# A two-layer decoder trunk: layer 0's small steps at fixed places between the large matmuls, large buffers at multiples of 512 bytes, and natural row order in the output projection

## The chip, the cores and the metric

The kernel runs on one core of a Trainium2 chip. The metric is the time of one execution in microseconds (us); less is better. A core has a matmul engine, TensorE (PE in the profile, with its weight loads on a row of their own, PEld), a vector engine (DVE), a scalar engine (ACT), GpSimd (POOL) and SyncE (SP), which here only issues DMAs. Matmuls read on-chip memory (128 partitions of bytes, in which each buffer has an address) and write to PSUM, a small memory in banks of 512 float32 values per partition.

## What is computed

256 tokens of width 2048 run through two layers. Layer 0 mixes tokens with two kinds of heads, whose inputs come from one projection of 6144 columns:

```python
proj = h @ w_in                      # columns: x, y (recurrence), q, f, v, g (heads), 1024 each
lru = rg_lru(causal_depthwise_conv(x), ...)      # h_t = a_t h_(t-1) + u_t, gates from 256-wide blocks
lru = lru * gelu(y)
hg = hgrn2(q, f, v, ...)             # 8 heads of 128; per-head RMSNorm; times silu(g)
mixed = concat(lru, hg) @ w_out      # 2048 x 2048
h = h + mixed
h = h + squared_relu(rms_norm(h) @ w1) @ w2      # 8192 wide
```

Layer 1 has a q/k/v projection, rotary angles on a quarter of each head, attention over three dilated windows merged into one weighted softmax, an output projection and the same MLP. A last RMSNorm follows. All is float32 in and out.

## The kernel before

**Precision.** A float32 operand is split into a high part (a cast on ACT, line 130 for weights) and a rest (a subtraction on DVE, line 131). Each product takes three matmuls: high by high, high activation by weight rest, activation rest by weight high. Activations are the stationary operand (128 tokens), 512 columns of weights stream past them.

**Units.** Weights come in units of 128 x 2048 values (1 MB) in a fixed order, listed at the start. `fetch` issues a unit's DMA on SP's queue into `raw` and its split into `hi` and `lo`; each of the three has three buffers. `unit` hands the next one to the matmuls. A unit of the input projection serves 24 matmuls: 4 row blocks, 2 halves of the tokens, 3 products. Most large products outside it (`blocks`) use a Strassen-like form with seven products in place of eight: combined activation blocks stand in `formx` (from bufa) and `formh` (from bufb), combined weights in `s` and `t`, and each block product has 48 matmuls on such blocks. The activations themselves are in `bufa` and `bufb` (four chunks of four row blocks).

**Order.** `ORDER` lists layer 0's steps: a letter and a number are one 512-column group of the input projection (`tokens_group`: four units, 96 matmuls, then two evictions on ACT into a tile `tk`, line 359), G0 and G1 are the recurrence's gates. Two heads at a time go through `hgrn`: transposes of q and f (line 435, PSUM tile pt), sigmoids, products (line 462, pd), eight doubling levels of a decayed product (lines 474 and 480, pl; DVE lines 483 to 501 between them), and the product with v (lines 508 to 510, po). `lru_in` transposes x and convolves it, `lru_gates` computes gates and scan, `lru_gelu` and `lru_out` apply the gelu branch and write rows 0 to 7 of bufb; `finish` normalises head outputs, applies silu(g) (lines 532, 534), transposes and writes rows 8 to 15 (lines 270, 271).

A scheduler of the framework orders each engine's instructions by a simulated time line, with priorities. Large matmuls and some transposes (`mm`, `turn`) are tied to their order in the code by `chain`; the small matmuls of the steps above are issued with plain calls, so the scheduler puts them among the large ones where it finds them ready. `HOOKS` says behind which unit of which group a whole function is recorded. `pt`, `pd` and `po` have one buffer each and all transposes of steps share pt.

**Output projection.** `out_project` multiplies bufb by w_out: the first 1024 columns plainly (row groups 0 to 3 of four row blocks each, in that order), the rest by `blocks`. Rows are taken in the order `PAIRED` (0, 2, 4, 6, 1, 3, 5, 7, then 8 to 15), so the first two groups need all recurrence rows. `mixed_forms` makes formh on the way. The heads' second `finish` is recorded behind the first unit.

**Layer 1** begins with `columns(0, ...)`, and `rotary` is recorded behind it: 16 small DVE operations and two sines.

**Memory.** Pools are laid one behind another. In the built program the large buffers xall, bufa, bufb, raw, hi and lo start 32 bytes past a multiple of 512, the tiles behind them (formx, formh, s, t, tk) 96 bytes past.

Of the kernel before, what the change touches and what calls it, by code (L numbers as in the profile page):

```python
# [10 lines left out]
F32 = mybir.dt.float32  # L11
# [30 lines left out]
def trunk_kernel(ctx, tc, head, x, xtok, cols, tab, masks, pos, fin, w_in, w_gate, w_out, w_qkv, w_o, w1, w2, out):  # L42
# [59 lines left out]
    units.extend((w_out, 4 * n + g) for n in range(2) for g in range(4))  # L102
# [249 lines left out]

    def tokens_group(step, rt=None, by_k=False, behind=()):
        steps[:] = HOOKS.get(step, ())
        ps = tokens(w_in, 4 * PLACE[step], bufa, by_k=by_k)
        v = vgs.tile([P, 2, 512], F32, name="tk", bufs=7)
        with urgent():
            for j in range(2):
                after(A.activation(v[:, j], ps[j], AF.Copy, scale=1.0 if rt is None else rt[:, j:j + 1]), behind)
        return v  # L360
# [15 lines left out]
    HOOKS = {}  # L376
# [50 lines left out]

    done = {"v0": vfirst}
    outs, roots = {}, {}

    def turned(tiles, at):
        p = psc.tile([P, 2, S], F32, name="pt", bufs=1)
        for i, (z, m) in enumerate(zip(tiles, at)):
            for j in range(2):
                T.transpose(p[:, i, j * P:j * P + P], z[:, j, m * P:m * P + P], ident)  # L435
        return p
# [4 lines left out]
    def hgrn(c2):  # L441
        g, at = c2 // 2, 2 * (c2 % 2)
        heads = (2 * c2, 2 * c2 + 1)
# [5 lines left out]
        p = turned([done[f"q{g}"]] * 2, (at, at + 1))  # L449
# [3 lines left out]
        p = turned([done[f"f{g}"]] * 2, (at, at + 1))  # L453
# [4 lines left out]
        pd = psc.tile([P, 2, 2, P], F32, name="pd", bufs=1)  # L458
        for h in range(2):
            for j in range(2):  # L460
                js = slice(j * P, j * P + P)
                T.matmul(pd[:, h, j], kq[:, h, js], qp[:, h, js], start=True, stop=True)  # L462
# [6 lines left out]
        while c <= 128:  # L469
            pl = psc.tile([P, 2, 2, 64], F32, name="pl", bufs=2)  # L470
            if c == 128:
                plf = pl.rearrange("p h j c -> p h (j c)")
                for h in range(2):
                    T.matmul(plf[:, h], kq[:, h, :P], qp[:, h, P:], start=True, stop=True)
                A.copy(st[:, :, 2], plf)
                break
            for h in range(2):
                for j in range(2):
                    js = slice(j * P, j * P + P)
                    T.matmul(pl[:, h, j], kq[:, h, js], halves(qp[:, h, js], c, True), start=True, stop=True)  # L480
# [22 lines left out]
            c *= 2  # L503
        vg = done[f"v{g}"]
        po = psc.tile([P, 2, 2, P], F32, name="po", bufs=1)
        for h in range(2):
            vs = slice((at + h) * P, (at + h) * P + P)
            T.matmul(po[:, h, 0], st[:, h, 0], vg[:, 0, vs], start=True, stop=True)
            T.matmul(po[:, h, 1], st[:, h, 2], vg[:, 0, vs], start=True, stop=False)
            T.matmul(po[:, h, 1], st[:, h, 1], vg[:, 1, vs], start=False, stop=True)  # L510
# [8 lines left out]
        A.copy(o, po)  # L519

    def finish(g, half):
# [14 lines left out]
        p = turned([outs[4 * g + at] for at in pair_], (0, 0))  # L536
        if g and not half:
            bufb.tiles[3] = act.tile([P, 4, 2 * S], F32R, name="bufb3")
        for i, at in enumerate(pair_):
            split_to(bufb[:, 8 + 4 * g + at], p[:, i], col("gn", 4 * g + at))  # L540

    xc = wk.tile([P, 8, S], F32, name="xc", bufs=1)

    def lru_in(n, half):
        b0 = 4 * n + 2 * half
        p = turned([done[f"x{n}"]] * 2, (2 * half, 2 * half + 1))
        for i in range(2):
            b = b0 + i
            A.activation(xc[:, b], p[:, i], AF.Identity, bias=col("conv_b", b), scale=col("conv_w", 24 + b))
            for t in range(3):  # L550
                V.scalar_tensor_tensor(xc[:, b, 3 - t:], p[:, i, :S - 3 + t], col("conv_w", 8 * t + b),
                                       xc[:, b, 3 - t:], op0=OP.mult, op1=OP.add)
        split_to(bufb[:, b0:b0 + 2], xc[:, b0:b0 + 2])

    def lru_gates(gp):
# [25 lines left out]
    def lru_gelu(n):  # L581
        y = done[f"y{n}"]
        q = outs[f"y{n}"] = vgs.tile([P, 2, 512], F32, name="tk", bufs=7)
        for j in range(2):
# [3 lines left out]
            V.tensor_tensor(y[:, j], y[:, j], q[:, j], OP.mult)  # L588

    def lru_out(n, half):  # L590
        b0 = 4 * n + 2 * half
        p = turned([done[f"y{n}"]] * 2, (2 * half, 2 * half + 1))
        z = outs[f"y{n}"][:, half].rearrange("p (i s) -> p i s", i=2)
        V.tensor_tensor(z, p, xc[:, b0:b0 + 2], OP.mult)
        split_to(bufb[:, b0:b0 + 2], z)

    do = lambda f, *args: lambda: f(*args)
# [12 lines left out]
    for step in ORDER.split()[1:]:  # L610
        if step[0] == "G":
# [18 lines left out]
    steps[:] = [[do(finish, 1, 0), do(finish, 1, 1)], [close_mixers]]  # L630
# [257 lines left out]
    nrm = out_project(w_out, "nmlp0", (0, 1, 2, 3))  # L888
# [6 lines left out]
    angles = {}  # L895

    def rotary():
        ppi = wk.tile([P, 2], I32, name="ppi", bufs=1)
        nc.gpsimd.dma_start(ppi, pos)
        ppf = wk.tile([P, 2], F32, name="ppf", bufs=1)  # L900
        ang = wk.tile([P, 2, 16], F32, name="ang", bufs=1)
        cosT = wk.tile([P, 2, 32], F32, name="cosT", bufs=1)
        sinT = wk.tile([P, 2, 32], F32, name="sinT", bufs=1)
        cos, sin = cosT[:, :, :16], sinT[:, :, 16:]
        after(V.tensor_copy(ppf, ppi), lastv)
        for j in range(2):
            V.tensor_scalar(ang[:, j], tab_[:, TC_FREQ:TC_FREQ + 16], ppf[:, j:j + 1], None, op0=OP.mult)
        MAGIC = 12582912.0
        V.tensor_scalar(cos, ang, 1.0 / (2.0 * math.pi), None, op0=OP.mult)
        V.tensor_scalar(cos, cos, MAGIC, None, op0=OP.add)  # L910
        V.tensor_scalar(cos, cos, MAGIC, None, op0=OP.subtract)
        rest = 2.0 * math.pi
        for bits in (5, 13, 21, None):
            part = rest if bits is None else math.floor(rest * 2.0 ** bits) / 2.0 ** bits
            rest -= part
            V.scalar_tensor_tensor(ang, cos, -part, ang, op0=OP.mult, op1=OP.add)
        PI = float(np.nextafter(np.float32(math.pi), np.float32(0)))
        V.tensor_scalar(cos, ang, math.pi / 2, None, op0=OP.add)
        V.tensor_scalar(sin, cos, math.pi, -2.0 * math.pi, op0=OP.is_gt, op1=OP.mult)
        V.tensor_tensor(cos, cos, sin, OP.add)  # L920
        V.tensor_scalar(cos, cos, PI, -PI, op0=OP.min, op1=OP.max)
        V.tensor_scalar(sin, ang, PI, -PI, op0=OP.min, op1=OP.max)
        lut(cos, cos, AF.Sin)
        lut(sin, sin, AF.Sin)
        A.copy(cosT[:, :, 16:], cos)
        V.tensor_scalar(sinT[:, :, :16], sin, -1.0, None, op0=OP.mult)
        angles.update(cos=cosT, sin=sinT)

# [128 lines left out]
    rotary()  # L1057
# [106 lines left out]
def _layout(a):  # L1164
# [21 lines left out]
    for g in range(0, 16, 4):  # L1186
# [7 lines left out]
    c = np.ascontiguousarray  # L1194
    return {
# [6 lines left out]
        "w_in": c(np.concatenate(w_in)), "w_gate": c(w_gate), "w_out": c(toks(n(a["rec_w_out"][0]), PAIRED)),  # L1202
# [21 lines left out]
```

## Time and profile before

| | |
|---|---|
| median of 3 runs | 2161.68 us (2159.28 to 2161.76) |
| the profiled execution, its own time | 2162.48 us |
| its span on the core | 2160.7 us, mean granted TensorE clock 0.996 |
| busy: PE, PEld, DVE, ACT | 99%, 82%, 82%, 61% of the span |
| matmuls | 9854, of 24875 instructions |
| DMA | 500.12 MB, 231 GB/s |

"Line engine op out<-in" names a group of instructions; numbers of buffers are left out. In a line of waits the engine, tile and line that waited stand first, then who ended the wait. "PEclk" in a window is the share of full TensorE clock that was granted. Matmuls overlap, so the start of one to the start of the next is the time that one takes; the duration shown beside it is longer.

### The profile page before, as it was taken

The page shows a single profiled execution, that of the slowest core. Times are in us where ns is not written, and L with a number is a line of the kernel's source. Part 1 is how long each engine was busy: PE and PEld are TensorE (multiplying, and loading weights), DVE is VectorE, ACT ScalarE, POOL GpSimd, SP SyncE. Part 2 cuts the span into 40 slices and gives each one's busy share as a digit, 9 for nine tenths or more (in the row PEclk, how much of TensorE's full clock was granted, in tenths as well). Part 3 has the DMA queues.
Part 4 walks back from the last instruction along what each step waited for, and adds up shares of the span by engine and source line. Part 5 has one row for each costly group of instructions (what it writes and reads, how often), then busy time and mean ns, then how long its engine had stood idle before and what let it go on. Part 6 is the DMA issues. An engine that isn't in the chain of part 4 may idle for free.

```text
span 2160.7 us, 24875 instructions
## 1 busy us (share of the span) xinstructions
PE 2140.7 (99%) x9854; PEld 1771.6 (82%) x9854; DVE 1781.6 (82%) x1687; ACT 1307.5 (61%) x1305; POOL 72.4 (3%) x89
## 2 busy tenths in 40 slices
PE   9999998999999999999999999999999999999998
PEld 8888887888888888888887888888888888888887
DVE  6566777988888888889898888798987988888887
ACT  6445575666566556557665666566755755755664
POOL 0000000000000000000000000000000000000000
PEclk9999999999999999999999999999999999999999
DMA  8544455778778887877787766667878778787885
GB/s 335 179 156 156 157 181 173 230 225 267 251 241 244 272 245 227 274 249 233 224 281 240 227 204 211 215 204 241 249 231 278 237 245 257 253 242 241 270 260 156
DMA packets 70165, 500.12 MB, mean 231 GB/s; under 512 B 7841, under 2 KB 8097, under 8 KB 10273
## 3 DMA queue, kind: packets, MB, share of 16 engines
q1 hardware_dynamic: 57888, 412.99, 50.8%
q0 software_dynamic: 11872, 84.94, 21.4%
q8 instruction: 77, 1.26, 0.2%
q10 hardware_dynamic: 288, 0.61, 0.1%
q14 instruction: 40, 0.32, 0.0%
HBM read 496.41 MB, written 2.10 MB: 231 GB/s over the span
## 4 chain that ended last, share of the span: by engine, by line
PE 97%; DVE 1%; DMA 1%; ACT 0%; issue 0%; DVEq 0%
PE p L221 62%; PE pd L221 14%; PE po L221 14%; PE pl L224 2%; PE pt L221 2%; PE pl L480 1%; PE pl L221 1%; DVE lo L131 0%; DMA raw<-in_w_qkv 0%; PE pt L435 0%; DMA both_in<-in_head 0%; ACT hi L130 0%; PE pd L462 0%; DVE s L159 0%; DVE ho L534 0%
## 5 line engine op out<-in xcount | busy, mean ns | idle before, releaser
L131 DVE TENSOR_TENSOR lo<-raw,hi 128x2048 fp32r<-128x2048 f32 (+1 forms) x364 | 788.9, 2171 | 248.3 <-ACT hi L130 246.2
L130 ACT CAST hi<-raw 128x2048 fp32r<-128x2048 f32 (+1 forms) x364 | 659.2, 1817 | 538.1 <-PE p L221 335.5
L221 PE MATMUL p<-hi,bufa 128*128 128x512 f32 x2000 | 641.1, 393 | 0.6 <-ACT bufa L270 0.6
L221 PEld LDWEIGHTS p<-hi,bufa 128*128 128x128 f32 x2000 | 375.7, 188 | 79.0 <-ACT bufa L270 0.9
L221 PE MATMUL p<-hi,bufb 128*128 128x512 f32 x1264 | 407.9, 393 | 0.0
L221 PE MATMUL p<-lo,bufa 128*128 128x512 f32 x1000 | 392.1, 392 | 1.1 <-DVE lo L131 1.1
L131 DVE TENSOR_TENSOR lo<-s,hi 128x2048 fp32r<-128x2048 f32 x120 | 274.2, 2285 | 12.7 <-ACT hi L130 10.5
L221 PEld LDWEIGHTS p<-hi,bufb 128*128 128x128 f32 x1264 | 238.3, 189 | 50.5
L130 ACT CAST hi<-s 128x2048 fp32r<-128x2048 f32 x120 | 228.9, 1907 | 54.3 <-PE po L221 23.3
L221 PE MATMUL p<-lo,bufb 128*128 128x512 f32 x632 | 247.0, 391 | 0.0
L221 PEld LDWEIGHTS p<-lo,bufa 128*128 128x128 f32 x1000 | 188.3, 188 | 40.6 <-DVE lo L131 1.6
L221 PEld LDWEIGHTS p<-lo,bufb 128*128 128x128 f32 x632 | 119.2, 189 | 25.1
L221 PE MATMUL p<-hi,formx 128*128 128x512 f32 x352 | 118.3, 397 | 0.0
L221 PE MATMUL pd<-hi,bufa 128*128 128x512 f32 x352 | 116.7, 393 | 0.0
L131 DVE TENSOR_TENSOR lo<-t,hi 128x2048 fp32r<-128x2048 f32 x40 | 91.5, 2287 | 17.6 <-ACT hi L130 17.6
L221 PE MATMUL po<-hi,bufb 128*128 128x512 f32 (+1 forms) x320 | 102.3, 386 | 0.0
L221 PE MATMUL p<-hi,formh 128*128 128x512 f32 x288 | 96.3, 395 | 0.0
L159 DVE TENSOR_TENSOR s<-s,raw 128x2048 f32<-128x2048 f32 x40 | 91.3, 2282 | 2.4 <-DMA raw<-in_w_qkv 2.4
L159 DVE TENSOR_TENSOR s<-raw,t 128x2048 f32<-128x2048 f32 x40 | 91.4, 2284 | 0.4 <-DMA raw<-in_w_o 0.3
L221 PE MATMUL po<-hi,bufa 128*128 128x512 f32 x256 | 84.9, 392 | 0.0
L130 ACT CAST hi<-t 128x2048 fp32r<-128x2048 f32 x40 | 76.2, 1906 | 12.6 <-PE pd L221 6.4
L221 PE MATMUL pd<-hi,bufb 128*128 128x512 f32 x256 | 83.0, 389 | 0.0
(303 smaller groups left out, 2800.3 us busy)
## 6 DMA issues: line engine op xcount, KB each, us to landing
raw<-in_w SPq DMA_DIRECT2D x224, 1024.0 KB, 6.7
raw<-in_w_in SPq DMA_DIRECT2D x45, 1024.0 KB, 4.9
raw<-in_w_qkv SPq DMA_DIRECT2D x42, 1024.0 KB, 6.7
t<-in_w SPq DMA_DIRECT2D x32, 1024.0 KB, 6.7
t<-in_w POOLq DMA_DIRECT2D x32, 1024.0 KB, 8.8
s<-in_w POOLq DMA_DIRECT2D x32, 1024.0 KB, 9.2
raw<-in_w_out SPq DMA_DIRECT2D x15, 1024.0 KB, 4.9
raw<-in_w_o SPq DMA_DIRECT2D x15, 1024.0 KB, 4.9
```

Of the source, the lines that this page charges most:

```text
L130: casts[:] = [after(A.copy(h, w), [])]
L131: i = V.tensor_tensor(l, w, h.bitcast(F32), OP.subtract)
L159: return V.tensor_tensor(held[to], held[x], held[y], OP.add)
L221: chain[:] = [after(T.matmul(*args, **kw), chain)]
L224: chain[:] = [after(T.transpose(out_, in_, ident), chain)]
L480: T.matmul(pl[:, h, j], kq[:, h, js], halves(qp[:, h, js], c, True), start=True, stop=True)
```

## The change

- **Fixed places.** All matmuls and transposes of the steps go through `mm` and `turn`, so their order among the large matmuls is the code's. The step functions become generators that stop (`yield`) between parts, `hgrn` at eleven places; in it `T.matmul` becomes `mm` and the tiles pt, pd and po become `bank`. They stand in four lanes (a and b: pairs of heads; c: the recurrence; d: finish), and `tokens` advances lanes behind every 12th matmul, as a table `TICKS` says.
- **PSUM.** Heads use pd or pt for all their tiles, by lane; recurrence and finish use po; every second gate uses pl in place of p.
- **Order.** The steps are v0 q0 f0 x0 q1 f1 v1 x1 G0 g0 y0 G1 y1 g1 (w_in is laid out to match). The reload of x goes ahead of g1.
- **Output projection.** The first 1024 columns of w_out keep natural row order, in row groups 0, 2, 1, 3: recurrence rows 0 to 3, heads 0 to 3, recurrence rows 4 to 7, heads 4 to 7. `mixed_forms` moves to fit; `finish` of the second half is in lane d, behind the first four twelves.
- **Rotary angles** are computed behind v0, in a tile that lies where `x_in` was; cos and sin tables stay in the constants' pool.
- **Addresses.** Padding of two tiles changes; with the two tables, the large buffers and the tiles behind them (formx, formh, s, t, tk, xc, st, qk) start at multiples of 512 bytes. Buffers and instructions are the same in number: 9621 matmul instructions as built, 8724 of them 512 wide.

```diff
-    units.extend((w_out, 4 * n + g) for n in range(2) for g in range(4))
+    units.extend((w_out, 4 * n + g) for n in range(2) for g in (0, 2, 1, 3))
-    c_ = cst.tile([P, NCOL + 48], F32, name="c_")[:, :NCOL]
+    c_ = cst.tile([P, NCOL + 34], F32, name="c_")[:, :NCOL]
-    ones = tmp.tile([P, S], F32, name="nr", bufs=1)[:, :P]
+    ones = tmp.tile([P, ONES], F32, name="nr", bufs=1)[:, :P]
     def tokens(src, i0, mov, kgs=(0, 1, 2, 3), by_k=False, behind=(), then=()):
-        ks = PAIRED if any(src is w for w in (w_out, w_o, )) else range(KB)
+        ks = PAIRED if src is w_o else range(KB)
...
-            for j, i in order:
+            for at_, (j, i) in enumerate(order):
...
                 mm(ps[j], xl, h, start=False, stop=last)
+                if at_ % 4 == 3 and ticks:
+                    tick(ticks.pop(0))
...
+    ticks, lanes = [], {}
+
+    def tick(which):
+        for name in which.strip("."):
+            with urgent():
+                while lanes[name] and next(lanes[name][0], True):
+                    lanes[name].pop(0)
...
     def tokens_group(step, rt=None, by_k=False, behind=()):
-        steps[:] = HOOKS.get(step, ())
+        ticks[:] = TICKS.get(step, "").split()
...
+    rotary()
     done = {"v0": vfirst}
-    def turned(tiles, at):
-        p = psc.tile([P, 2, S], F32, name="pt", bufs=1)
+    def turned(name, tiles, at):
+        p = psc.tile([P, 2, S], F32, name=name, bufs=1)
...
-                T.transpose(p[:, i, j * P:j * P + P], z[:, j, m * P:m * P + P], ident)
+                turn(p[:, i, j * P:j * P + P], z[:, j, m * P:m * P + P])
     def hgrn(c2):
         g, at = c2 // 2, 2 * (c2 % 2)
+        bank = "pt" if at else "pd"
...
+        yield
...
-            both_p = pmm.tile([P, 512], F32, name="p")
+            both_p = psc.tile([P, 512], F32, name="pl", bufs=2) if m % 2 else pmm.tile([P, 512], F32, name="p")
...
-    HOOKS.update({
-        "x0": [[do(hgrn, 0)], [], [do(hgrn, 1)]],
-        "q1": [[do(lru_in, 0, 0)], [], [do(lru_in, 0, 1)]],
-        "x1": [[do(hgrn, 2)], [], [do(hgrn, 3)]],
-        "y0": [[], [do(lru_in, 1, 0)], [], [do(lru_in, 1, 1)]],
-        "y1": [[do(lru_gelu, 0)], [do(finish, 0, 0)], [do(lru_out, 0, 0)], [do(lru_out, 0, 1), do(finish, 0, 1)]],
-        "g1": [[do(lru_gelu, 1)], [do(reload)], [do(lru_out, 1, 0)], [do(lru_out, 1, 1)]],
-    })
+    lanes.update(a=[hgrn(0), hgrn(2)], b=[hgrn(1), hgrn(3)],
+                 c=[lru_in(0, 0), lru_in(0, 1), lru_in(1, 0), lru_in(1, 1),
+                    lru_gelu(0), lru_out(0, 0), lru_out(0, 1), lru_gelu(1), lru_out(1, 0), lru_out(1, 1)],
+                 d=[finish(0, 0), finish(0, 1), finish(1, 0), finish(1, 1)])
     for step in ORDER.split()[1:]:
+        if step == "g1":
+            reload()
...
-    steps[:] = [[do(finish, 1, 0), do(finish, 1, 1)], [close_mixers]]
+    ticks[:] = TICKS["o0"].split()
+    steps[:] = [[], [], [close_mixers]]
...
-            then = () if not whole else ((((), (0,), (1,), (2,)), ((), (), (3,), ())) if src is w_out else
+            then = () if not whole else ((((), (), (0, 1), (2,)), ((), (3,), (), ())) if src is w_out else
...
-    nrm = out_project(w_out, "nmlp0", (0, 1, 2, 3))
+    nrm = out_project(w_out, "nmlp0", (0, 2, 1, 3))
...
-ORDER = "v0 q0 f0 x0 v1 q1 f1 x1 G0 y0 g0 G1 y1 g1"
+ORDER = "v0 q0 f0 x0 q1 f1 v1 x1 G0 g0 y0 G1 y1 g1"
+TICKS = {
+    "f0": ". . . . . a b .",
+    "x0": "a b a b a b a b",
+    "q1": "a b a b a b a b",
+    "f1": "ac bc ac bc ac bc a b",
+    "v1": "a b a b a b a b",
+    "x1": "a b a b a b a b",
+    "g0": "ac bc ac bc ac bc . .",
+    "y0": "d d d d . . . .",
+    "y1": "c . c . c . c .",
+    "g1": ". c c . c . c .",
+    "o0": "d d d d . . . .",
+}
+ONES = 240
-"w_out": c(toks(n(a["rec_w_out"][0]), PAIRED)),
+"w_out": c(np.concatenate([toks(wo[:, :1024]), toks(wo[:, 1024:], PAIRED)])),
```

More of the change, by code (lines that the diff above doesn't have):

```diff
@@ L426, in trunk_kernel, with rotary @@
     V.tensor_scalar(omlb, lb, -1.0, 1.0, op0=OP.mult, op1=OP.add)
+    angles = {}
+    def rotary():
+        room = wk.tile([P, 128], F32, name="room", bufs=1)
+        ppi, ppf = room[:, :2].bitcast(I32), room[:, 2:4]
+        ang = room[:, 32:64].rearrange("p (j c) -> p j c", j=2)
+        nc.gpsimd.dma_start(ppi, pos)
+        cosT, sinT = (cst.tile([P, 2, 32], F32, name=name) for name in ("cosT", "sinT"))
+        cos, sin = cosT[:, :, :16], sinT[:, :, 16:]
+        V.tensor_copy(ppf, ppi)
+        for j in range(2):
+            V.tensor_scalar(ang[:, j], tab_[:, TC_FREQ:TC_FREQ + 16], ppf[:, j:j + 1], None, op0=OP.mult)
+        MAGIC = 12582912.0
+        V.tensor_scalar(cos, ang, 1.0 / (2.0 * math.pi), None, op0=OP.mult)
+        V.tensor_scalar(cos, cos, MAGIC, None, op0=OP.add)
+        V.tensor_scalar(cos, cos, MAGIC, None, op0=OP.subtract)
+        rest = 2.0 * math.pi
+        for bits in (5, 13, 21, None):
+            part = rest if bits is None else math.floor(rest * 2.0 ** bits) / 2.0 ** bits
+            rest -= part
+            V.scalar_tensor_tensor(ang, cos, -part, ang, op0=OP.mult, op1=OP.add)
+        PI = float(np.nextafter(np.float32(math.pi), np.float32(0)))
+        V.tensor_scalar(cos, ang, math.pi / 2, None, op0=OP.add)
+        V.tensor_scalar(sin, cos, math.pi, -2.0 * math.pi, op0=OP.is_gt, op1=OP.mult)
+        V.tensor_tensor(cos, cos, sin, OP.add)
+        V.tensor_scalar(cos, cos, PI, -PI, op0=OP.min, op1=OP.max)
+        V.tensor_scalar(sin, ang, PI, -PI, op0=OP.min, op1=OP.max)
+        lut(cos, cos, AF.Sin)
+        lut(sin, sin, AF.Sin)
+        A.copy(cosT[:, :, 16:], cos)
+        V.tensor_scalar(sinT[:, :, :16], sin, -1.0, None, op0=OP.mult)
+        angles.update(cos=cosT, sin=sinT)
+    rotary()
     done = {"v0": vfirst}
     outs, roots = {}, {}
-    def turned(tiles, at):
-        p = psc.tile([P, 2, S], F32, name="pt", bufs=1)
+    def turned(name, tiles, at):
+        p = psc.tile([P, 2, S], F32, name=name, bufs=1)
         for i, (z, m) in enumerate(zip(tiles, at)):
             for j in range(2):
-                T.transpose(p[:, i, j * P:j * P + P], z[:, j, m * P:m * P + P], ident)
+                turn(p[:, i, j * P:j * P + P], z[:, j, m * P:m * P + P])
         return p
@@ L457, in hgrn @@
             A.activation(f[:, h], f[:, h], AF.Identity, scale=omlb[:, hd:hd + 1], bias=lb[:, hd:hd + 1])
-        pd = psc.tile([P, 2, 2, P], F32, name="pd", bufs=1)
+        yield
+        pd = psc.tile([P, 2, 2, P], F32, name=bank, bufs=1)
         for h in range(2):
@@ L461, in hgrn @@
                 js = slice(j * P, j * P + P)
-                T.matmul(pd[:, h, j], kq[:, h, js], qp[:, h, js], start=True, stop=True)
+                mm(pd[:, h, j], kq[:, h, js], qp[:, h, js], start=True, stop=True)
         st = wk.tile([P, 2, 3, P], F32, name="st", bufs=2)
@@ L473, in hgrn @@
                 for h in range(2):
-                    T.matmul(plf[:, h], kq[:, h, :P], qp[:, h, P:], start=True, stop=True)
+                    mm(plf[:, h], kq[:, h, :P], qp[:, h, P:], start=True, stop=True)
                 A.copy(st[:, :, 2], plf)
@@ L503, in hgrn @@
             c *= 2
+        yield
         vg = done[f"v{g}"]
[L505 removed]
+        po = psc.tile([P, 2, 2, P], F32, name=bank, bufs=1)
         for h in range(2):
             vs = slice((at + h) * P, (at + h) * P + P)
[L508 to L510 removed]
+            mm(po[:, h, 0], st[:, h, 0], vg[:, 0, vs], start=True, stop=True)
+            mm(po[:, h, 1], st[:, h, 2], vg[:, 0, vs], start=True, stop=False)
+            mm(po[:, h, 1], st[:, h, 1], vg[:, 1, vs], start=False, stop=True)
         if not at:
@@ L519, in hgrn @@
         A.copy(o, po)
+        yield
     def finish(g, half):
@@ L894, in trunk_kernel @@
     wk = mixers.enter_context(tc.tile_pool(name="wk2", bufs=2))
[L895 to L927, printed above, removed]
     def rope(t):
```

25 lines of the change are left out of this document (15 added, 10 removed).

## The prediction

> **What bounds the kernel now.** I read the page first (span, busy shares, chain), then TensorE's waits, then the granted clock in 2 us windows, then the timeline of single matmuls. From the page, the span, the engines and the chain of waits by engine:
>
> ```profile
> span 2160.7 us, 24875 instructions
> PE 2140.7 (99%) x9854; PEld 1771.6 (82%) x9854; DVE 1781.6 (82%) x1687; ACT 1307.5 (61%) x1305; POOL 72.4 (3%) x89
> ...
> PE 97%; DVE 1%; DMA 1%; ACT 0%; issue 0%; DVEq 0%
> ```
>
> TensorE is the bound: 97% of the chain. A change can only win by taking out its pauses, or by making its matmuls follow each other faster. The pauses (us in total, times, longest):
>
> ```profile
> PE pt L435 <- DVE bufb L271: 5.0, 1, 5.0
> PE pl L480 <- DVE xall L498: 1.7, 2, 0.9
> PE pt L435 <- DVE tk L594: 1.1, 1, 1.1
> PE p L221 <- DVE lo L131: 1.1, 1, 1.1
> ...
> PE p L221 <- ACT bufb L252: 0.9, 1, 0.9
> ```
>
> All but the fourth lie in layer 0, which the change rearranges. The two L435 ones are one place, where the last recurrence outputs and head outputs are transposed just ahead of the output projection. Windows there (us, PE busy, count, granted clock, DMA share, GB/s), then the timeline:
>
> ```profile
> 334.00:336.00 2.00, 0.00 (x0) 0.54 0.43 115
> ...
> 346.00:350.00 4.00, 4.00 (x21) 1.00 0.00 0
> ```
> ```profile
> 330.30 0.60 PE L435 MATMUL pt<-tab__183,ho 128*128 128x128 f32 x4
> 330.66 0.48 PE L221 MATMUL p<-hi,bufb 128*128 128x512 f32 x1
> ...
> 331.21 0.40 PE L221 MATMUL p<-hi,bufb 128*128 128x512 f32 x1
> ...
> 336.58 1.09 PE L435 MATMUL pt<-tab__183,tk 128*128 128x128 f32 x4 [4.97 <-DVE bufb L271]
> 338.80 1.11 PE L435 MATMUL pt<-tab__183,tk 128*128 128x128 f32 x4 [1.14 <-DVE tk L594]
> ...
> 344.63 0.39 PE L221 MATMUL p<-lo,bufb 128*128 128x512 f32 x1
> ```
>
> The pause costs more than its 5.0 + 1.1 us: the clock falls to half (0.54 of it on average in the first window) and is full again after some ten slow matmuls.
>
> The second thing is the pitch of matmuls, start to start. The same weights stream over two kinds of stationary operand: activations in bufa, and the combined blocks in formx. From the timeline (start, duration, count):
>
> ```profile
> 609.30 0.40 PE L221 MATMUL pd<-hi,formx 128*128 128x512 f32 x1
> ...
> 614.89 0.39 PE L221 MATMUL p<-hi,bufa 128*128 128x512 f32 x1
> ...
> 616.74 0.62 PE L221 MATMUL p<-hi,bufa 128*128 128x512 f32 x2
> ...
> 625.00 0.61 PE L221 MATMUL p<-hi,bufa 128*128 128x512 f32 x2
> ...
> 631.12 0.39 PE L221 MATMUL pd<-hi,bufa 128*128 128x512 f32 x1
> ```
>
> From 609.30 to 614.89 stand 24 matmuls on formx: 232.9 ns each. From 625.00 to 631.12 stand 27 on bufa: 226.7 ns. Just behind formx, bufa too is slow: eight from 614.89 to 616.74, 231.3 ns. In the built program bufa, bufb and the weights (hi, lo) start 32 bytes past a multiple of 512, formx and formh 96 past. That distance of 64 bytes is the only difference between the streams that I can name, besides where in the memory they lie.
>
> **The change, part by part.**
>
> *The place before the output projection.* From 331.21 to 344.63 there are 13.42 us. In it stand 11 full-width matmuls (2.49 us at 226.7 ns) and three groups of transposes at 0.36 us each (330.30 to 330.66) with some 0.09 us of restart, 1.35 in all. So 9.6 us are lost there, waits and half clock together. The change gives L435's four users PSUM banks by kind (heads pd and pt, recurrence and head outputs po) and puts lru_out of the second half behind the 60th and 84th matmul of g1, 36 and 12 ahead of g1's end. The natural row order lets the output projection take row groups 0, 2, 1, 3, so recurrence rows 4 to 7 are wanted third and heads 4 to 7 last. That takes the place off the path: −9.6. With L480's 1.7 and the gates' 0.9 (those steps get fixed distances of 24 matmuls, 5.4 us, and the gates alternate two PSUM banks): −12.2, between −8 and −12.2.
>
> *Interruptions.* The built program has 13 more places in layer 0 where a group of small matmuls stands between large ones. One such place:
>
> ```profile
> 222.63 1.00 PE L480 MATMUL pl<-xall 128*128 128x64 f32 x8
> 223.44 0.48 PE L221 MATMUL p<-hi,bufa 128*128 128x512 f32 x1
> 223.75 0.40 PE L221 MATMUL p<-lo,bufa 128*128 128x512 f32 x1
> ```
>
> The matmul behind it takes 0.31 instead of 0.23 us: 13 × 0.09 = +1.2. The small matmuls are the same in number.
>
> *New waits at fixed places.* TensorE now stands still if a step's data is late; behind it queue the large matmuls, and behind those the casts on ACT and DVE that wait for a weight buffer, three deep, so a short wait shifts them and does not multiply. The steps of a head follow at 24 matmuls; the vector work between is a third of that. Three places are tight. The second finish step (transposing head outputs) stands 24 matmuls = 5.4 us behind the end of g0, and again of g1. Its chain, in the built program's order on ACT and DVE, goes by these rows:
>
> ```profile
> 289.11 1.28 ACT L252 ACT_TABLE_LOAD   x1
> 290.40 1.71 ACT L252 ACTIVATE bufb<-bufb,sp 128x256 f32<-128x256 f32 x4
> 292.01 1.90 ACT L130 CAST hi<-raw 128x2048 fp32r<-128x2048 f32 x1
> ...
> 329.92 0.68 ACT L359 ACTIVATE tk<-p,nr 128x512 f32<-128x512 f32 x1
> 332.38 0.72 ACT L252 ACTIVATE g<-tk 128x256 f32<-128x256 f32 x2
> ```
> ```profile
> 37.32 2.29 DVE L131 TENSOR_TENSOR lo<-raw,hi 128x2048 fp32r<-128x2048 f32 x1
> ...
> 333.84 0.75 DVE L532 TENSOR_TENSOR g<-g,tk 128x256 f32<-128x256 f32 x2
> ...
> 334.91 1.13 DVE L534 SCALAR_TENSOR_TENSOR ho<-ho,hr,g 128x128 f32<-128x128 f32 x4
> ```
>
> Behind g0: eviction 0.2 + 0.68, a cast 1.90 (to 2.8), table load 1.28, sigmoids 0.72 (to 4.8); DVE does lo meanwhile (2.8 to 5.1), then 0.75 + 1.13: ready at 7.0, wanted at 5.4, wait 1.5 us. Behind g1 no table load, but an eviction may come 1 us late: the same 1.5. The third is lru_out behind the 60th matmul of y1: ACT has the gates' sigmoids, three table loads, three casts and some twenty passes of 0.43 us (1.71 for four) ahead of the gelu, about 20.5 us plus DVE's product, against 19.4 on TensorE: up to 2. Together +5, between 0 (ACT runs ahead of this order) and +12 (the three at 2.5, and 0.08 us at each of the other 57 places). I add no half clock, by the window that holds layer 1's wait of 1.1 us (us; busy of PE, PEld, DVE, ACT, POOL; clock; DMA share; GB/s):
>
> ```profile
> 1000.00:1200.00 200.00, 198.87 (x894) 163.36 (x893) 178.53 (x170) 129.10 (x120) 8.35 (x10) 1.00 0.78 244
> ```
>
> The clock stayed at 1.00 there.
>
> *The rotary angles* move from the start of layer 1 to behind v0. There they stood ahead of a lo for which TensorE waited 1.1 us:
>
> ```profile
> 1152.11 0.36 DVE L907 TENSOR_SCALAR ang<-tab__183,ppf 128x16 f32<-128x16 f32 x2
> ...
> 1153.05 2.29 DVE L131 TENSOR_TENSOR lo<-raw,hi 128x2048 fp32r<-128x2048 f32 x1
> ```
>
> 0.94 us less ahead of it: −0.9 (0 to −1.1). At the new place 15 small DVE operations go ahead of the lo at 37.32. What that lo has to spare:
>
> ```profile
> 5.88 72.90 PE p L221 x312
> ```
>
> 312 matmuls are 13 units of 24; at 226.7 ns they would take 70.7, so a cold 2.2 us lies at the start and unit 6 begins at 5.88 + 2.2 + 6 × 5.44 = 40.7. Its lo ended at 39.6; 1.1 us and one matmul to spare. At the 0.19 us that five of them took at layer 1 (0.94), 15 in one chain would take 2.8 and cost 1.7; but they stand among two other chains of small operations there, and fill the gaps between dependent ones: I take 0 (0 to +1.7). The position's DMA is issued by POOL, which has nothing else before the output projection; the sine's table load only moves. The reload of x moves ahead of g1's loads on SP; in the built program it stands among the loads for y0 and waits for the heads' last use of xall, at the third and fourth fixed place of g0; the weight loads queued behind it wait for buffers that come free about then, and three units of lead lie between them and TensorE: 0.
>
> *Addresses.* In the changed program bufa, bufb, hi, lo, formx and formh all start at multiples of 512. All matmuls on formx and formh (windows over the whole span, for each tile alone) are then in the position towards the weights that bufa has now:
>
> ```profile
> 0.00:2161.00 2161.00, 260.02 (x1056) 1.00 0.72 231
> 0.00:2161.00 2161.00, 211.23 (x864) 1.00 0.72 231
> ```
>
> 1,056 + 864 = 1,920, times 6.2 ns: −11.9. The slow start behind them (8 × 4.6 ns = 0.037 us) stands at three changes in each of 40 block products, up to 4.4; some have transposes between, which slow the start anyway: −3. Together −15, between 0 (position isn't the cause) and −16.3. I take nearly the whole: it is the same instruction, clock and moving operand, and formx and formh, 33 KB apart, share the pitch.
>
> [...]
>
> *Sum:* −12.2 + 1.2 + 5 − 0.9 − 15 = −21.9. The profiled execution took 2162.48 (span 2160.7 and 1.8 around it), 0.8 above the median of 2161.68; against the median that is 2139.8: **2140 us**.
>
> **Rivals.**
> 1. *Addresses do nothing*: the 6.2 ns belong to the high place of formx and formh, not to the 64 bytes. For it: nothing in the trace has another offset at the same place. Against: two buffers far apart with one pitch. −6.9 remain: 2155.
> 2. *The 32 bytes cost too.* If 64 bytes past cost 6.2 ns, the 32 that bufa and all weights have now might cost 3.1: 3.1 ns for each of the 1,920 and of the 6,800 full-width matmuls on bufa and bufb (counted in rival 3) is 27 us more: 2113. Against: bufa and the weights have the same offset, and what differs may only be the distance between them. [...]
> 3. *Slower, by addresses*: 0 is a bad position, and the streams on bufa and bufb get the 6.2 ns that formx has, which keeps its own.
>
> ```profile
> 0.00:2161.00 2161.00, 957.74 (x4056) 1.00 0.72 231
> 0.00:2161.00 2161.00, 678.78 (x2964) 1.00 0.72 231
> ```
>
> These are bufa's and bufb's matmuls; some 220 of the 7,020 are narrow, 6,800 are full: 6,800 × 6.2 = +42, less 6.9: 2197. It decides as soon as the pitch on bufa rises by 2 ns (13.6 us with formx unimproved).
> 4. *Slower, by fixed places*: the step of a head waits each time, because DVE's order puts a lo of 2.29 us ahead of it. About 60 places; at 0.5 us each 30 instead of 5: 2165. It decides from 27 us of waits in all. Against: 5.4 us between the steps of one head.
>
> **How the numbers follow.** Forecast 0.62, rival 1 0.13, rival 2 0.12, rival 3 0.07, rival 4 0.06. Runs of this kernel differ by 0.1%, so 0.2% (4.3 us) is what can be told from no change. The forecast's own range is 2131 to 2149 (waits 0 to 12, addresses 0.8 to 1.1 of the term). Downward it reaches to rival 2, 2107; upward past rival 1 with its waits at the upper end, 2163. Faster: 0.62 + 0.12 + most of rival 1 = 0.82. Same: the rest of rival 1 and a mild rival 4, 0.05. Slower: 0.13.
>
> **What would show it.** Right: no wait over 2.5 us on TensorE in layer 0, the clock at 1.00 from 10 to 2150 us, the pitch on formx and formh at 226.7, on bufa unchanged, the 1.1 us wait at layer 1's start gone. Wrong: a pitch on formx still near 233 (rival 1), on bufa below 224 or above 229 (rivals 2 and 3), or waits of TensorE in layer 0 of over 12 us (rival 4).

## The result, and the profile after

The changed kernel takes 2153.51 us (median of 7 runs, 2152.77 to 2155.61), the kernel before 2161.0 in the same session (7 runs): 0.9969 of it, with a 95% interval of 0.9957 to 0.998. It is faster by 7.5 us. The forecast was 2140, a gain of 21.9: the direction is right, two thirds of the gain are missing.

The page of the changed kernel: span, busy time of the engines, chain of waits by engine.

```profile
span 2151.5 us, 24903 instructions
...
PE 2127.6 (99%) x9854; PEld 1770.5 (82%) x9854; DVE 1781.4 (83%) x1687; ACT 1307.3 (61%) x1305; POOL 72.3 (3%) x89
...
PE 95%; ACT 2%; DVE 1%; DMA 1%; issue 0%; SPq 0%; DVEq 0%; ACTq 0%
```

TensorE is still the bound, but ACT now has 2% of the chain, where it had 0. First to where the time came from. The timeline of the changed kernel gives the first matmul on formx, 24 matmuls on formx up to the next on bufa, and the last matmul of 512 columns; then the first and the last row of the kernel before.

```profile
436.90 0.39 PE L221 MATMUL p<-hi,formx 128*128 128x512 f32 x1
...
612.73 0.39 PE L221 MATMUL pd<-hi,formx 128*128 128x512 f32 x1
...
618.17 0.39 PE L221 MATMUL p<-hi,bufa 128*128 128x512 f32 x1
...
2140.14 0.39 PE L221 MATMUL po<-hi,bufb 128*128 128x512 f32 x1
```
```profile
431.74 0.40 PE L221 MATMUL p<-hi,formx 128*128 128x512 f32 x1
...
2149.24 0.39 PE L221 MATMUL po<-hi,bufb 128*128 128x512 f32 x1
```

From the first formx matmul to the last one of 512 columns the kernel before took 1717.5 us, the changed one 1703.2: 14.3 less. The pitch on formx is 5.44 / 24 = 226.7 ns; on bufa it stays at that (24 matmuls from 618.17 to the next on formx at 623.61). But the changed kernel reaches its first formx matmul at 436.9 instead of 431.7: what lies ahead of it in layer 0 ("the first part" from here on) was to be 6 us shorter and is 5.2 longer. TensorE's waits in the changed kernel show why (us in total, times, longest):

```profile
PE p L221 <- ACT bufb L252: 5.2, 4, 2.2
PE po L224 <- DVE xc L602: 3.2, 1, 3.2
PE pl L221 <- ACT bufb L252: 2.3, 4, 0.6
PE p L221 <- DVE lo L131: 1.8, 1, 1.8
...
PE po L224 <- DVE tk L641: 1.2, 2, 0.9
...
PE po L224 <- DVE ho L583: 0.5, 1, 0.5
```

The 5.0 and 1.1 us ahead of the output projection are gone, and so are L480's. The first and the third row, 7.5 us, are new: the gates, once at G0 and once at G1. There TensorE waits for ACT (L252 is the line of the sigmoid). The timeline of the changed kernel at G0: the first gate matmul, the second gate of the first block, that of the second block, and the first matmul of g0.

```profile
216.89 0.49 PE L221 MATMUL p<-bufb,hi 128*128 128x256 f32 x2
...
219.72 0.51 PE L221 MATMUL p<-bufb,hi 128*128 128x256 f32 x2 [1.88 <-ACT bufb L252]
...
222.03 0.80 PE L221 MATMUL pl<-bufb,hi 128*128 128x256 f32 x2 [0.56 <-ACT bufb L252]
...
230.46 0.63 PE L221 MATMUL p<-hi,bufa 128*128 128x512 f32 x1
```

Each second gate waits until ACT has read the first: both stand in halves of one PSUM bank (run 3 below tests that this is the reason). At the first block ACT comes late, since a cast stands ahead of the sigmoid (ACT in the timeline of the changed kernel).

```profile
216.86 1.89 ACT L130 CAST hi<-raw 128x2048 fp32r<-128x2048 f32 x1
...
219.19 0.47 ACT L252 ACTIVATE bufb<-p,c__91 128x256 f32<-128x256 f32 x1
```

In the kernel before, the same bank was shared, but the scheduler had put the heads' small matmuls into these gaps (timeline of the kernel before, at G0):

```profile
206.13 1.00 PE L480 MATMUL pl<-xall 128*128 128x64 f32 x8
```

The new table of places names no place in G0 and G1, so there is nothing to fill them. And from 222 us on the matmuls are slow. Windows of 3.41 us of the changed kernel (us, PE busy, count, granted clock, DMA share, GB/s):

```profile
217.84:221.25 3.41, 1.53 (x13) 1.00 0.00 0
221.25:224.67 3.42, 2.85 (x14) 0.50 0.75 247
...
231.49:234.91 3.42, 3.42 (x10) 0.50 0.01 2
234.91:238.32 3.41, 3.41 (x23) 1.00 0.77 235
245.15:248.56 3.41, 1.59 (x10) 1.00 0.95 339
248.56:251.97 3.41, 1.99 (x11) 1.00 1.01 418
```

Behind a window that was busy for 1.53 us the clock is at exactly half for four such windows. The 3.24 us wait for the convolution, from 246.74 to 249.98, is longer, but falls into two windows, and the clock stays whole.

### The profile page after: what moved, and what is told of

It is laid out like the page before. It is cut to its first block, busy times and chain, and to the rows that moved or that the text cites. A ratio compares the mean times of both kernels' runs of the same rounds, so it can differ in the third digit from the quotient of the medians.

```text
span 2151.5 us, 24903 instructions
## 1 busy us (share of the span) xinstructions
PE 2127.6 (99%) x9854; PEld 1770.5 (82%) x9854; DVE 1781.4 (83%) x1687; ACT 1307.3 (61%) x1305; POOL 72.3 (3%) x89
## 4 chain that ended last, share of the span: by engine, by line
PE 95%; ACT 2%; DVE 1%; DMA 1%; issue 0%; SPq 0%; DVEq 0%; ACTq 0%
PE p L221 60%; PE pd L221 15%; PE po L221 14%; PE pl L224 2%; PE pt L221 2%; PE pl L221 2%; DVE lo L131 1%; ACT hi L130 1%; DMA raw<-in_w_qkv 0%; ACT bufb L252 0%; DMA both_in<-in_head 0%; PE po L224 0%; ACT L252 0%; ACT bufa L270 0%; DVE bufb L630 0%
## 5 line engine op out<-in xcount | busy, mean ns | idle before, releaser
L221 PE MATMUL p<-hi,bufa 128*128 128x512 f32 x2000 | 650.8, 395 | 0.4 <-ACT bufa L270 0.4
```

The costliest lines, as they stand in the source:

```text
L221: chain[:] = [after(T.matmul(*args, **kw), chain)]
```

## The experiments

My theory at this point: the addresses are worth about 14 us; the fixed places removed what they were to remove, but at the gates they opened waits which, with the half clock, cost about 13. The rival: the addresses are worth little, and layer 0 gave the 7.5.

### 1 and 2. Addresses alone, each way

The kernel before, with two pads changed, so that all large buffers start at multiples of 512:

```diff
-    c_ = cst.tile([P, NCOL + 48], F32, name="c_")[:, :NCOL]
+    c_ = cst.tile([P, NCOL + 40], F32, name="c_")[:, :NCOL]
-    ones = tmp.tile([P, S], F32, name="nr", bufs=1)[:, :P]
+    ones = tmp.tile([P, 240], F32, name="nr", bufs=1)[:, :P]
```

> The kernel before with nothing changed but two pads, so that bufa, bufb, hi, lo, formx and formh start at multiples of 512 bytes. Theory (addresses are worth about 14 us, and the new layer 0 costs the rest of them back): the pitch on formx and formh falls from 233.4 to 226.7 ns, layer 0 is as before (first formx matmul at 431.7 us), and the time is 2161.0 - 14.4 = about 2146.5. Rival (the addresses are worth little and the 7.5 us came from the new layer 0): pitch 233.4 still, time 2161.

Measured: 2146.62 us, 0.993 of the kernel before (0.9918 to 0.9942). Its timeline:

```profile
431.55 0.39 PE L221 MATMUL p<-hi,formx 128*128 128x512 f32 x1
...
607.38 0.39 PE L221 MATMUL pd<-hi,formx 128*128 128x512 f32 x1
...
612.81 0.39 PE L221 MATMUL p<-hi,bufa 128*128 128x512 f32 x1
```

The first part takes as long as before (431.55 against 431.74), and the 24 formx matmuls take 5.43 us, 226.3 ns each. And the changed kernel with the old offsets:

```diff
-    c_ = cst.tile([P, NCOL + 34], F32, name="c_")[:, :NCOL]
+    c_ = cst.tile([P, NCOL + 42], F32, name="c_")[:, :NCOL]
-ONES = 240
+ONES = 256
```

> The changed kernel with the old offsets (bufa, bufb, hi and lo 32 bytes past a multiple of 512, formx and formh 96 past), all else as changed. Theory: pitch on formx and formh back at 233.4 ns, bufa and bufb unchanged, first formx matmul at 436.9 as in the changed kernel, time 2153.5 + 14.4 = about 2168, slower than the kernel before by 7. Rival (layer 0 gave the gain): 2153.5, faster than before by 7.5.

Measured: 2168.87 us, 1.0033 of the kernel before (1.0021 to 1.0045).

```profile
616.64 0.40 PE L221 MATMUL pd<-hi,formx 128*128 128x512 f32 x1
...
622.24 0.39 PE L221 MATMUL p<-hi,bufa 128*128 128x512 f32 x1
```

5.60 / 24 = 233.3 ns. Without the addresses the change makes the kernel slower by 7 us. By the medians the addresses are worth 15.2 us in the kernel before and 15.4 in the changed one, so the rival is out. One part of the expectation missed: the first formx matmul stands at 439.08 us, not at 436.9, because the wait for the convolution is 3.5 us here and 3.41 us at half clock follow it. The wait at layer 1's start is 1.7 us shorter, so the two nearly cancel, which is luck; from the first formx matmul to the very last matmul the difference is 13.3 us, and 15.0 if the two waits are taken as equal.

### 3. A bank for each gate

```diff
-            both_p = psc.tile([P, 512], F32, name="pl", bufs=2) if m % 2 else pmm.tile([P, 512], F32, name="p")
...
-                p = both_p[:, gate * S:gate * S + S]
+                p = (psc.tile([P, 512], F32, name="pl", bufs=2) if gate else pmm.tile([P, 512], F32, name="p"))[:, :S]
```

> The changed kernel with a PSUM bank for each gate of a block (the first gate in a bank of p, the second in one of pl) in place of one bank for both. Theory (the second gate's matmuls wait for the sigmoid that reads the first gate's half of the same bank, and these waits threw the clock to half at the first gates): the waits at the two gate places, 3.6 and 3.9 us, go, and with them the half clock from 222 to 234 us, worth about 5.5: 2153.5 - 13 = about 2140.5. Rival A (the half clock has another cause): only the waits go, 2146. Rival B (ACT is late anyway and TensorE then waits for it at the next bank or at the next fixed place): 2150 or more.

Measured: 2142.33 us, 0.9916 (0.9903 to 0.9928). G0 in its timeline, and one row of its waits:

```profile
216.64 0.49 PE L221 MATMUL p<-bufb,hi 128*128 128x256 f32 x2
...
222.66 0.40 PE L221 MATMUL p<-hi,bufa 128*128 128x512 f32 x1
```
```profile
PE po L224 <- DVE xc L602: 5.1, 1, 5.1
```

The gates take 6.02 us instead of 13.57; at G1 a single wait of 0.24 is left. So it is the sharing that makes these waits. (Each gate now has a tile of its own as well as a bank; the run doesn't tell the two apart.) Part of the gain comes back 14 us later: TensorE now reaches the convolution's place in g0 sooner, and the wait there, where the bank po is still being read by the first half's convolution on VectorE, grows from 3.24 to 5.14 us, with 6.8 us at half clock from 240.1 on. The time is 1.8 us above the theory's number, and this return is the likely reason.

The two halves of the bank have different addresses, and still the second gate waits for the reader of the first: 1.88 and 0.56 us in the changed kernel's rows above.

### 4. The convolution two places later

```diff
-    "g0": "ac bc ac bc ac bc . .",
+    "g0": "a b ac bc ac bc c c",
```

> The changed kernel with the four-place sequence of the convolution's second half in g0 put two places (24 matmuls) later. Theory (the 3.24 us wait at the fourth place of g0 is VectorE still busy with the gates' work just ahead of it): the wait goes, 2153.5 - 3.2 = about 2150.3. Rival (VectorE is behind throughout g0): the wait stays over 2 us, time 2153.

Measured: 2152.65 us, 0.9948 (0.9936 to 0.996), but the six runs lie apart: 2145.98 and 2146.80 with a mean granted clock of 0.998, and four from 2152.55 to 2153.98 with 0.992 or 0.993. The profile is of the latter kind. In it the wait for the convolution is gone (one of 1.1 us stands at the finish step of y0, where 0.5 was), but now both gate places run at half clock, G1 too:

```profile
286.00:289.41 3.41, 1.18 (x10) 1.00 0.77 296
289.41:292.82 3.41, 2.85 (x14) 0.50 0.21 55
```

So the wait can be moved away, but the median doesn't tell what that is worth: whether the gates' waits halve the clock differs from execution to execution. The run prices the half clock instead. A stretch of 13.65 us at half clock would by itself take the mean clock of an execution down by 0.003, so by this estimate the two executions at 0.998 had none at the gates, and the four at 0.992 or 0.993 had two, as the profile of one of them (0.992) shows. The two groups lie 6.8 us apart: an estimate of 3.4 us of the whole time for each place.

### 5. All of it together

Runs 3 and 4 in one kernel, and the steps of y0 and y1 a little further apart:

```diff
-    "y0": "d d d d . . . .",
-    "y1": "c . c . c . c .",
+    "y0": "d . . d d . . d",
+    "y1": "c c . . . c . c",
```

> The changed kernel with a bank for each gate, the convolution's second half two places later in g0, the finish steps of y0 at every 36th matmul in place of every 12th, and the gelu of y1 at its first two places with the products two places behind the old ones. Theory: of the 2142.3 us that the banks alone gave, the 5.14 us wait for the convolution goes with the half clock behind it (some 2 us), and the small waits of y0 and y1 (1.6 us): about 2133.5. Rival (VectorE is late through g0 and the wait only moves to the finish step of y0): 2139 or more.

Measured: 2132.78 us (4 runs, 2131.75 to 2135.57), 0.9868 (0.9855 to 0.9882): faster than both kernels, and 0.7 from the expectation. Two rows of its waits, its first formx matmul, and the stretch from just ahead of G0 to the output projection as one window:

```profile
PE p L221 <- DVE lo L131: 1.6, 1, 1.6
...
PE pl L221 <- ACT bufb L252: 0.2, 1, 0.2
```
```profile
416.34 0.39 PE L221 MATMUL p<-hi,formx 128*128 128x512 f32 x1
```
```profile
214.00:345.00 131.00, 130.83 (x667) 1.00 0.56 199
```

TensorE stands still for 0.17 us in 131, at full clock. Against run 1, with equal addresses, the first part is 431.55 - 416.34 = 15.2 us shorter. Some 2 us of that are not the change but the start: in the windows from 6 to 8 and from 8 to 10 us run 1 has 5 and 6 matmuls, run 5 has 8 and 10, and from 10 to 12 us they have 10 and 11. At half the rate for 4 us run 1 loses 2, by this estimate.

### 6. The gaps filled instead

The gates keep their shared banks, but four of the heads' places go between the two gates of a block, as the scheduler of the kernel before had it:

```diff
+                if ticks and not gate:
+                    tick(ticks.pop(0))
...
-    "g0": "ac bc ac bc ac bc . .",
+    "G0": "a b a b",
+    "g0": "ac bc c c c c . .",
```

> The changed kernel with the shared gate banks as they are, but with four of the heads' fixed places taken out of g0 and put between the two gates of a block at G0, where the scheduler of the kernel before had put such groups. Theory (the gate waits of the kernel before were as long, and filled by those groups): the waits at G0 fall from 3.6 us to 1.5 or less, the half clock there goes, and the time is 2153.5 - 2 - 5 = about 2146. Rival A (the work lost in g0 and gained in G0 evens out, and ACT and VectorE get later): 2151 or more. Rival B (waits go, half clock stays): 2151.

Measured: 2151.43 us, 0.9953 (0.994 to 0.9965). At G0 the waits fall from 3.56 to 1.28 us (1.04, 0.12, 0.12) and the clock stays whole there. But TensorE then waits 5.3 us for VectorE at the convolution's place, with two windows at half clock behind it:

```profile
PE po L224 <- DVE hr L322: 5.3, 1, 5.3
```

That is rival A: the time is given back where VectorE is late. It shows that small groups do fill the gates' waits; the 2 us that are left as a gain can't be told from none (the intervals overlap).

### 7. The rotary angles back at layer 1

The call of `rotary` stands behind `columns(0, ...)` again, with its first operation tied behind the eviction as before.

> The changed kernel with the rotary angles computed at the start of layer 1 again. Theory (their 0.9 us of small VectorE operations stood ahead of the lo that TensorE waits for at the start of layer 1, and what made the wait longer after the change is that TensorE comes sooner against the load of raw): the wait at layer 1's start grows from 1.83 to about 2.7 us, the time by 0.9 to 2154.4, which the median can hardly show. Rival (these operations cost nothing at either place): the wait stays at 1.8.

Measured: 2155.34 us, 0.9972 (0.9961 to 0.9982), which is little more than the changed kernel's 2153.51 (the ranges overlap); the wait is 3.22 us, 0.5 above the expectation. VectorE in the timeline of this run, then of the changed kernel:

```profile
1153.31 2.29 DVE L159 TENSOR_TENSOR s<-s,raw 128x2048 f32<-128x2048 f32 x1 [3.83 <-DMA raw<-in_w_qkv]
...
1156.46 2.29 DVE L131 TENSOR_TENSOR lo<-raw,hi 128x2048 fp32r<-128x2048 f32 x1
```
```profile
1149.80 2.29 DVE L159 TENSOR_TENSOR s<-s,raw 128x2048 f32<-128x2048 f32 x1 [3.46 <-DMA raw<-in_w_qkv]
...
1152.01 2.29 DVE L131 TENSOR_TENSOR lo<-raw,hi 128x2048 fp32r<-128x2048 f32 x1
```

From the landing of raw to the lo that TensorE wants there are 3.15 us with the angles and 2.21 without: 0.94 us, as forecast. What that is worth in time isn't shown: with the angles in their new place the wait was 0.12 us in run 2, 0.27 in run 4, 1.62 in run 5 and 1.83 in the changed kernel. That it hangs on how TensorE stands to the DMA is my reading, and no run tests it by itself.

### 8 to 11. Which distance costs

First everything at 96 past a multiple of 512 (`NCOL + 58` in place of `NCOL + 34`):

> The changed kernel with all of bufa, bufb, raw, hi, lo, formx and formh at 96 bytes past a multiple of 512. Theory (the distance between the stationary operand and the weights, modulo some power of two, sets the pitch): 226.7 ns on all of them, time 2153.5. Rival (96 past a multiple of 512 is a bad place in itself): 233.4 ns on all of them, 8,700 matmuls x 6.7 ns = 58 us more, 2212.

Measured: 2154.94 us, 0.9968 (0.9957 to 0.998). Its formx stretch:

```profile
614.75 0.39 PE L221 MATMUL pd<-hi,formx 128*128 128x512 f32 x1
...
620.19 0.39 PE L221 MATMUL p<-hi,bufa 128*128 128x512 f32 x1
```

5.44 / 24 = 226.7 ns: 96 is no bad place; the distance between the two operands decides, not where each lies. Then formx and formh alone, moved by 32, 128 and 256 bytes (`ONES` 248, 272, 304), one run each, with the kernel before at 2161.32:

> The changed kernel with formx and formh at 32 bytes past a multiple of 512, bufa, bufb, hi and lo at 0. Theory (what costs is that the distance from the stationary operand to the weights is not a multiple of 512): a pitch between 226.7 and 233.4 ns on formx and formh, 230 by half of the step at 64 bytes, and 226.7 on bufa and bufb; time 2153.5 + 1,920 x 3.3 ns = 2160. Rival (only the 64-byte step costs, a distance of 32 is free): 226.7 everywhere, 2153.5.

> The changed kernel with formx and formh at 128 bytes past a multiple of 512, bufa, bufb, hi and lo at 0. Theory (every distance that is not a multiple of 512 costs): 233 ns or more on formx and formh, 2166 or more. Rival (a distance of 64 is a bad one among others, and multiples of 128 are free): 226.7, 2153.5.

> The changed kernel with formx and formh at 256 bytes past a multiple of 512, bufa, bufb, hi and lo at 0. Theory (every distance that is not a multiple of 512 costs): 233 ns or more on formx and formh, 2166 or more. Rival (multiples of 256 are free): 226.7, 2153.5.

The formx stretches of run 9 (32 bytes) and run 11 (256 bytes):

```profile
617.38 0.39 PE L221 MATMUL pd<-hi,formx 128*128 128x512 f32 x1
...
622.98 0.39 PE L221 MATMUL p<-hi,bufa 128*128 128x512 f32 x1
```
```profile
611.47 0.39 PE L221 MATMUL pd<-hi,formx 128*128 128x512 f32 x1
...
616.91 0.39 PE L221 MATMUL p<-hi,bufa 128*128 128x512 f32 x1
```

A distance of 32 costs as much as one of 64: 5.60 / 24 = 233.3 ns and 2167.45 us, so the half step I expected isn't there. 128 bytes: 232.9 ns (24 matmuls from 616.61 to 622.20) and 2167.74 us. 256 bytes: 226.7 ns and 2150.56 us. My theory said 512, which is refuted for 256; what the runs show is that 0 and 256 are free and 32, 64 and 128 are not. Why, they don't show. Runs 9 to 11 are one execution each, so their times say less than their pitches. (In run 11's execution the gates kept the full clock: only 3.41 us, behind the convolution's wait, were at half, where the profiled execution of the changed kernel had 13.65. That goes with its 2150.56.)

Run 8 also shows the half clock from the other side. At G0 it has the waits of the changed kernel, 1.88 and three of 0.56 us, but they fall into the windows in another way; at G1 they don't:

```profile
215.78:219.19 3.41, 2.36 (x18) 1.00 0.54 228
219.19:222.60 3.41, 2.02 (x14) 1.00 0.13 17
...
287.45:290.87 3.42, 1.41 (x11) 1.00 0.58 242
290.87:294.28 3.41, 2.85 (x14) 0.50 0.49 151
```

From the first gate matmul to g0's first matmul (217.18 to 227.59 in its timeline) G0 takes 10.41 us here and 13.57 in the changed kernel. To that come the 4.45 us that the changed kernel runs at half clock behind it, 2.2 of them lost: the half clock costs 5.4 us there. Not all of it is gained where it is absent. Run 8 reaches the convolution's place sooner, waits 5.1 us for VectorE there instead of 3.24, and has 3.41 us at half clock behind that. In the whole time run 4 puts it at 3.4 us a place.

## Why the prediction was wrong, step by step

*The place before the output projection*, −9.6, and L480's −1.7: the waits went. With the new waits mended (run 5 against run 1) the first part gains 15.2 us, where −12.2 and +1.2 made 11.0. Some 2 of the other 4.2 are the start at half clock, up to 1.7 the half clock at the gates of the kernel before, below; the remainder I didn't trace.

*The gates*, −0.9: this step failed. I argued that "the gates alternate two PSUM banks". They do, by block: in the code it is every second block, and not every second gate as I described the change, that uses pl. The two gates of one block still share a bank, and nothing is left to stand between them. Waits of 1.2 us (0.91, 0.14 and 0.12 at G1 of the kernel before) became 7.5, so this term is +6.3 where it was −0.9. The price is a little over the waits: at full clock G0 takes 10.41 us with them (run 8) and 6.02 without (run 3), 4.4 less for 3.56 us of waits.

*"I add no half clock"*: failed too. I took it from one wait of 1.1 us behind which the clock stayed whole. The profile of before held the opposite case, at its own gates, with two waits of 0.78 and 0.91 us:

```profile
272.70:276.12 3.42, 1.73 (x13) 1.00 0.17 69
276.12:279.53 3.41, 3.27 (x16) 0.50 0.63 216
```

That was the row to quote. In the changed kernel the half clock cost 5.4 us at G0.

*Interruptions*, +1.2: the number of places is as forecast (the timelines have 50 ahead of the first formx matmul before and 63 after). No run measures the price of one apart from the rest.

*New waits elsewhere*, +5: the sum was right, by luck, since the list was not. The finish steps and lru_out took 0.5 and 1.2 us; 3.24 lay at a place that I hadn't named, where lru_in's second transposes need the bank that the first half's convolution on VectorE still reads, while VectorE has the gates' products and a lo to do.

*The rotary angles*, −0.9: the 0.94 us on VectorE are right, but the time didn't come: the wait at that place was to go and grew from 1.1 to 1.83 us, so the term is +0.7.

*Addresses*, −15: right, 15.2 us alone by the medians (run 1). In the changed kernel 14.3 lie behind the first formx matmul, with the 0.7 of the rotary angles' place in them, so 15.0. Run 9's 32 bytes and run 10's 128 cost as much as the 64: 6.6 and 6.2 ns a matmul.

*The sum.* The two profiled executions tell where it went. The first part was to be 6.0 us shorter and is 5.2 longer, 11.2 too much: 7.2 from the gates (+6.3 for −0.9) and 5.4 from the half clock, less about 1.7 that the kernel before lost at half clock at its own gates, which the forecast hadn't counted; the 0.3 left over is not an exact account, since the start at half clock favours the changed kernel by some 1.7 (a 512-column matmul took 0.43 us up to 9.9 us in the kernel before, and 0.24 from 6.25 us on in the changed one) and each wait costs a little more than its length. The rest was to be 15.9 shorter and is 14.3: the 1.6 are the rotary angles. Together that is 12.8 of the 13.7 between 2139.8 and 2153.5; the last 0.9 is how the profiled executions stand to the medians.

*The range.* Its two conditions (waits 0 to 12, addresses 0.8 to 1.1 of the term) give 2133.5 to 2150 and not 2131 to 2149; 2153.5 lies outside both.

*The signs.* Of those for right, the two on the pitch came true and three didn't: a wait of 3.24 us, the half clock, and layer 1's wait. Of those for wrong, rival 4's came true, just: the waits in layer 0 come to 12.4 us by the rows shown above, over its 12.

*The rivals.* Addresses that do nothing (1), 32 common bytes that cost (2) and a bad place at 0 (3) are refuted by runs 1, 8 and the pitch on bufa. That the time is close to rival 1's 2155 is chance: its cause is out. Rival 4 had the right kind of cause, too many waits at fixed places, but looked for it at the heads' steps; most of it was at two places that had no table entry at all, with a price that came to a good part from the clock.

## What to carry to other kernels

When an automatic order is replaced by a written one, list what the old order had put into each wait, above all where a stage gets no entry in the new table. Here two short results shared a PSUM bank and the second waited for the reader of the first, 7.5 us in all, where one wait of 0.24 was left with a bank for each (run 3): give each its own before counting on alternation. A wait that is taken out of one place can come back at the next one where another engine is late, so mend them together (runs 3, 4 and 5). Try stationary and moving operands at equal offsets modulo 256 bytes: here two pads brought the pitch on formx from 232.9 ns to 226.3 and were worth 0.7% (run 1).

## What the hardware showed that I had not expected

- The pitch of a 512-column matmul was 226.3 to 226.7 ns where stationary operand and weights differed by 0 bytes (both at 0, 32 or 96 past a multiple of 512) or by 256 (256 against 0), and 232.9 to 233.3 ns where they differed by 32, 64 or 128 (32 and 128 against 0, 96 against 32).
- Stretches at half clock in layer 0 lasted 3.41 us (the kernel before, at its gates), 6.8 (run 3, at the convolution's place), 10.24 (the kernel before, ahead of the output projection) or 13.65 (the changed kernel, G0), one to four times 3.41. In windows of that length, counted from where a stretch begins, the clock fell to half behind one busy for 1.53 us (the changed kernel), 1.41 (run 8), 1.18 (run 4), 0.87 and 1.73 (the kernel before); it did not behind 1.59, 1.69 and 1.99 (the changed kernel), 2.02 and 2.36 (run 8). 1.69 without and 1.73 with a fall show that busy time as the profile counts it doesn't decide alone. At half clock, windows busy for 0.98 and 2.27 us (the kernel before) and for 2.85 (the changed kernel, the gates with their waits) were followed by another at half, those of 3.27 and 3.42 by full clock. The length of one wait doesn't decide alone either: in the changed kernel 1.88 us inside one window stood ahead of half clock, 3.24 us across two did not.
- Matmuls didn't come at full rate from the start, and not from the same time in each execution: the kernel before took 0.43 us for each of 512 columns up to 9.9 us and 0.23 behind it, the changed kernel 0.24 from 6.25 us on, and from 6 to 8 us run 9 has 5 matmuls and run 10 has 9. The same four waits at G0 were followed by half clock in the changed kernel (behind a window busy for 1.53 us) and by full clock in run 8 (2.36 and 2.02). That the place of the windows differs from execution to execution as the start does is my reading, and no run tests it.
